# Scan stage of a two-layer hybrid backbone: loads and SiLUs issued from the scan steps

## The chip, the cores and the metric

The kernel is one program on one core of a Trainium2 chip. The metric is the device time of that core in microseconds (us), lower is better. The runs shown are whole executions; one further execution was recorded by the profiler, and every row below comes from that one.

## What is computed

Two layers over 1024 latent tokens and 256 context tokens, width 1024. Each layer projects the normed tokens into four mixers of 256 columns, concatenates their outputs, projects them back (`w_out`), and runs a squared-ReLU MLP. Only the mixers matter here:

```python
y_conv = silu(layer_norm(depthwise_conv(a * sigmoid(g)))) @ w_pw + b_pw
y_gla  = rms_norm(bidirectional_scan(gla)) * silu(r)
y_att  = softmax_attention(q, k, v)
y_ret  = rms_norm(bidirectional_scan(retention)) * silu(g)
x = x + g1 * (concat([y_conv, y_gla, y_att, y_ret]) @ w_out)
```

The second layer needs no context outputs, so its stage below has 8 token tiles of 128 and not 10.

## The kernel before, in words

All matrices are kept transposed, 128 features on the partitions and tokens along the free axis. A product in full precision is made of three products of halves (`mm3`, lines 190 to 195): `split` (line 180) casts a tile to a high half on ScalarE (line 181) and leaves the rest as a low half on VectorE (line 182). The program is Python that writes out every instruction; a scheduler then orders each engine's instructions by their place in the program and by when it reckons their inputs to be ready, so a load may be issued ahead of its place. All loads named here go through the one queue of SyncE (SP), in order.

**The scan stage** (lines 952 to 1112, once per layer) lies between the projections, which leave their results in DRAM, and the `w_out` matmuls. It runs as follows.

- `zc` (128 x 2 x 1280) holds the normed convolution outputs, `gt` (128 x 4 x 1280) the gates: columns 0 and 1 those of the gated linear attention (GLA, "g"), columns 2 and 3 those of the retention ("r"). `y[t]` collects the four mixers' outputs of token block t; its columns 4 and 5 are the attention's.
- Lines 971 to 984 allocate and load constants (`mc`, on POOL's queue, line 974) and the chunk states of both scans (`kvs`: `gkv`, `rkv`, line 982). Each of these tiles has one buffer (`bufs=1`).
- `states("g")` (line 986, drained at line 1012) is the serial recurrence over tiles: 16 VectorE operations at line 994 and four at line 999 that give `gs`, the decayed state that every GLA tile reads. `states("r")` does the same for the retention beside the scan.
- `scan_loads` (line 1005) loads one tile's queries and keys (`gx` or `rx`, line 1008) and values (`gv` or `rv`, line 1009), three buffers each; line 1013 issues the first three ahead. Line 1015 loads and splits the pointwise weights `pw`.
- Lines 1016 to 1026 issue the loads of `gt` columns 0 and 1, of `zc`, of `gt` columns 2 and 3, and of the attention outputs into `y[t][:, 4:6]`. Lines 1027 to 1036 apply SiLU to all of them but the attention's, on ScalarE (`act`, line 167, is the helper; the instruction is at line 175). `act` puts a table load ahead whenever the function wanted is in another table set than the last one: SiLU is in one set, the Ln and Exp of the tails in another.
- `scan_tile` (line 1038) does one tile: score matmuls into `sc`, a mask on VectorE (`gab`, lines 1054 and 1055; `rab`, line 1057), then into `oo` the products with the values and with the states. `scan_tail` (line 1079) norms a finished token block (ScalarE lines 1084, 1085 and 175, VectorE lines 1094 and 1096), multiplies by the gate and writes `y`.
- `pointwise` (line 954) splits 256 tokens of `zc` at a time (`shi`, `slo`), multiplies by `w_pw` and writes `y[t][:, 0:2]` (line 968).
- Line 1111 runs three streams in lockstep rounds, one step of each per round: the scans (GLA blocks first, then retention), `states("r")` and `pointwise()`. A block of n tiles takes n + 2 rounds, so the scans take 32 rounds in the first layer and 24 in the second; `pointwise` takes 10 and 8, from the first round on.

After the stage `w_out` (from line 1121) splits `y` and multiplies; its weight slabs (512 KB each) are loaded and split during the stage when queue and buffers allow.

Of the kernel before, what the change touches and what calls it, by code (L numbers as in the profile page):

```python
# [8 lines left out]
F32 = mybir.dt.float32  # L9
F32R = mybir.dt.float32r  # L10
I32 = mybir.dt.int32
AF = mybir.ActivationFunctionType
ALU = mybir.AluOpType
# [7 lines left out]
NTILE = NT // 128  # L21
CT = NCTX // 128
# [6 lines left out]
TOK = [(0, 256), (256, 512), (768, 512)]  # L29
# [45 lines left out]
CST, OFF = _consts()  # L75
# [25 lines left out]
def build(tc, a, out, dbg=None):  # L101
    cst = a["cst"]
    nc = tc.nc
# [33 lines left out]
    def cslice(name):  # L137
        o, n = OFF[name]
        return cst[:, o:o + n]
# [9 lines left out]
    glav = dram.tile([NTILE, 128, 256], F32, name="glav")  # L149
    glaf = dram.tile([NTILE, 128, 6, 128], F32, name="glaf")  # L150
    glakv = dram.tile([NTILE, 128, 128], F32, name="glakv")
    retv = dram.tile([NTILE, 128, 256], F32, name="retv")
    retf = dram.tile([128, 5, NT], F32, name="retf")
    retkv = dram.tile([NTILE, 128, 128], F32, name="retkv")
    yconv = dram.tile([128, 2, NT], F32, name="yconv")
    attraw = dram.tile([NTILE, 128, 320], F32, name="attraw")
    yatt = dram.tile([128, 2, NT], F32, name="yatt")
    gatedr = dram.tile([128, 4, NT], F32, name="gatedr")
# [8 lines left out]
    def act(out_, in_, func, want=None, **kw):  # L167
        if want == "anyexp":
            want = cur["set"] if cur["set"] in ("exp", "tanh") else "exp"
        if want is not None and want != cur["set"]:  # L170
            ld = nc.scalar.preload_act_table_set(sets[want]).ins
            for u_ in cur["users"]:
                after_(ld, u_)
            cur.update(set=want, users=[], load=ld)
        i_ = nc.scalar.activation(out_, in_, func, **kw).ins  # L175
        if want is not None:
            after_(i_, cur["load"])
            cur["users"].append(i_)

    def split(hi, lo, src):  # L180
        nc.scalar.copy(hi, src)  # L181
        nc.vector.tensor_tensor(lo, src, hi.bitcast(F32), op=ALU.subtract)  # L182
# [7 lines left out]
    def mm3(ps, pairs):  # L190
        n = len(pairs)
        for i, (lh, ll, rh, rl) in enumerate(pairs):
            mm(ps, lh, rh, i == 0, False)
            mm(ps, lh, rl, False, False)
            mm(ps, ll, rh, False, i == n - 1)

    def par(*streams):
        streams = [(iter(g), w, []) for g, w in streams]
        busy = True
        while busy:  # L200
            busy = False
            for gens, w, live in streams:
                while len(live) < w:
                    g = next(gens, None)
                    if g is None:
                        break
                    live.append(g)
                for g in list(live):
                    busy = True
                    if next(g, par) is par:  # L210
                        live.remove(g)
            yield
# [17 lines left out]
    def drain(g):  # L230
        for _ in g:
            pass
# [18 lines left out]
    def load_slab(src, k, n):  # L251
        wd_ = W["width"]
        st = W["st"].tile([128, wd_], F32, tag="wst", name="wst", bufs=W["stages"])
        if not isinstance(src, list):
            src = [(src, n)]
        o = 0
        v = st[:, :k * n].rearrange("p (k n) -> p k n", k=k)
        for s, w in src:
            nc.sync.dma_start(out=v[:, :, o:o + w], in_=s)
            o += w  # L260
        p = W["pools"][W["n"] // W["group"] % len(W["pools"])]
        W["n"] += 1
        hi = p.tile([128, wd_], F32R, tag="whi", name="whi")
        lo = p.tile([128, wd_], F32R, tag="wlo", name="wlo")
        split(hi[:, :k * n], lo[:, :k * n], st[:, :k * n])
        return (hi[:, :k * n].rearrange("p (k n) -> p k n", k=k), lo[:, :k * n].rearrange("p (k n) -> p k n", k=k))
# [20 lines left out]
    gdec = cpool.tile([128, NTILE, 2, 2], F32, name="gdec")  # L287
# [16 lines left out]
    def vec(l, name, i=0):  # L304
        o, _ = VROWS[name]
        return vecs[l][:, o + i:o + i + 1]
# [118 lines left out]
    b = bank()  # L425
# [43 lines left out]
    for l in range(2):  # L469
        last = l == 1  # L470
        tts = [1, 2] if last else [0, 1, 2]
# [194 lines left out]
        def tiles_of(t):  # L666
            o, n = TOK[t]
            return range(o // 128, (o + n) // 128)
# [75 lines left out]
        for half in range(2):  # L744
            sl = granule(l, [(C_CONV + 128 * half, 128), (C_CONV + 256 + 128 * half, 128)], 256)
            for t in tts:
                o, n = TOK[t]
# [10 lines left out]
        for q, c0 in enumerate((C_GATE_R, C_GATE_G)):  # L758
            sl = granule(l, [(c0, 256)], 256)
            for t in tts:  # L760
                o, n = TOK[t]
                for j in range(2):
                    b = colA(sl, j * 128, t)
# [178 lines left out]
        y = [None if last and t == 0 else xy_tile(t, "y") for t in range(3)]  # L942
# [4 lines left out]
        def bank2(tag):  # L947
            return psm.tile([128, 2, 512], F32, tag=tag, name=tag, bufs=2)

        open_w()  # L950
        mp = pools.get("mp", side="right", bufs=2, reuse_waits="tile")
        zc = mp.tile([128, 2, NT], F32, name="zc", bufs=1)
        gt = mp.tile([128, 4, NT], F32, name="gt", bufs=1)
        def pointwise():
            whi, wlo = pw
            for t in tts:
                for c in range(0, TOK[t][1], 256):
                    o = TOK[t][0] + c
                    shi = mp.tile([128, 2, 256], F32R, tag="shi", name="shi")
                    slo = mp.tile([128, 2, 256], F32R, tag="slo", name="slo")  # L960
                    split(shi, slo, zc[:, :, o:o + 256])
                    yield
                    bb = bank2("sc")
                    for d in range(2):
                        b = bb[:, d, :]
                        ds = slice(d * 128, (d + 1) * 128)
                        mm3(b[:, 0:256], [(whi[:, k, ds], wlo[:, k, ds], shi[:, k, :], slo[:, k, :]) for k in range(2)])
                        nc.scalar.activation(y[t][:, d, c:c + 256], b[:, 0:256], AF.Identity, bias=vec(l, "conv_b_pw", d))
                    yield

        mc = {}
# [14 lines left out]
        def states(nm):  # L986
            kv = kvs[nm]
            if nm == "g":
                nc.vector.tensor_tensor(gtot, gdec[:, :, :, 0], gdec[:, :, :, 1], op=ALU.mult)
            for n_ in range(1, NTILE - 1):  # L990
                for d_, od in enumerate((fwd, back)):
                    i, pr = od[n_], od[n_ - 1]
                    dec = gtot[:, i, d_:d_ + 1] if nm == "g" else mc["retdec"]
                    nc.vector.scalar_tensor_tensor(kv[:, i, d_, :], kv[:, pr, d_, :], dec, kv[:, i, d_, :],
                                                   op0=ALU.mult, op1=ALU.add)
                yield
            if nm == "g":
                for d_, i0, i1, p0 in ((0, 1, NTILE, 0), (1, 0, 1, 1), (1, 2, NTILE - 1, 3), (1, NTILE - 1, NTILE, 0)):
                    nc.vector.tensor_tensor(gs[:, i0:i1, d_, :], kv[:, p0:p0 + i1 - i0, d_, :],
                                            gdec[:, i0:i1, d_, d_:d_ + 1].to_broadcast([128, i1 - i0, 64]), op=ALU.mult)  # L1000
                yield
# [3 lines left out]
        def scan_loads(kind, i):  # L1005
            x = mp.tile([128, 6 if kind == "g" else 5, 128], F32, tag=kind + "x", name=kind + "x", bufs=3)
            v = mp.tile([128, 256], F32, tag=kind + "v", name=kind + "v", bufs=3)
            nc.sync.dma_start(out=x, in_=glaf[i] if kind == "g" else retf[:, :, i * 128:(i + 1) * 128])
            nc.sync.dma_start(out=v, in_=(glav if kind == "g" else retv)[i])
            ready[kind, i] = (x, v)  # L1010
# [5 lines left out]
        for q in range(0, 4, 2):  # L1016
            for t in tts:
                o, n = TOK[t]
                nc.sync.dma_start(out=gt[:, q:q + 2, o:o + n], in_=gatedr[:, q:q + 2, o:o + n])
            if q == 0:  # L1020
                for t in tts:
                    o, n = TOK[t]
                    nc.sync.dma_start(out=zc[:, :, o:o + n], in_=yconv[:, :, o:o + n])
        for t in tts:
            o, n = TOK[t]
# [75 lines left out]
        def scans():  # L1101
            for kind in ("g", "r"):
                for t in tts:
                    old = tails.pop() if tails else iter(())
                    for _ in scan_block(kind, t):
                        step(old)
                        yield
                    drain(old)
            drain(tails.pop())

        drain(par(([scans()], 1), ([states("r")], 1), ([pointwise()], 1)))
        pools.close("psm", "mp")
        if "y" in dbg and dbg.get("l", 0) == l:
            for t in tts:
# [156 lines left out]
```

## Time and profile before

| | us |
|---|---|
| three runs | 3226.3, 3220.46, 3217.87 |
| their median | 3220.46 |
| profiled execution, its own time | 3216.42 |
| its span, first to last instruction | 3214.7 |

The span is 1.7 us shorter than that execution's own time, and the execution is 4.0 us below the median. In the span the first layer's scan stage lies between about 645 and 755 us, the second's between about 2301 and 2402 us. "PEclk" in a row is the granted TensorE clock as a share of full speed; "DMA share" is how busy the 16 DMA engines were.

### The profile page before, as it was taken

The page shows a single profiled execution, that of the slowest core. Times are in us where ns is not written, and L with a number is a line of the kernel's source. Part 1 is how long each engine was busy: PE and PEld are TensorE (multiplying, and loading weights), DVE is VectorE, ACT ScalarE, POOL GpSimd, SP SyncE. Part 2 cuts the span into 40 slices and gives each one's busy share as a digit, 9 for nine tenths or more (in the row PEclk, how much of TensorE's full clock was granted, in tenths as well). Part 3 has the DMA queues.
Part 4 walks back from the last instruction along what each step waited for, and adds up shares of the span by engine and source line. Part 5 has one row for each costly group of instructions (what it writes and reads, how often), then busy time and mean ns, then how long its engine had stood idle before and what let it go on. Part 6 is the DMA issues. An engine that isn't in the chain of part 4 may idle for free. (4 is left out here: it accounts for less than half of the span.)

```text
span 3214.7 us, 43493 instructions
## 1 busy us (share of the span) xinstructions
PE 3026.1 (94%) x18101; PEld 2446.6 (76%) x18101; DVE 1671.4 (52%) x2660; ACT 913.3 (28%) x1650; POOL 66.6 (2%) x114
## 2 busy tenths in 40 slices
PE   7899899968999999999999799999779999999998
PEld 4777677646888888888888777687548888888887
DVE  5549634344655444454545659643444644444545
ACT  5223344243321111121112433343342321112222
POOL 0200000000000000000000010000000000000000
PEclk8899999979999999999999799999879999999999
DMA  8322412262122222221110310212531211111111
GB/s 273 112 70 86 129 44 79 84 216 95 60 79 86 86 86 79 82 63 40 40 40 1 99 55 30 80 48 65 174 117 70 66 46 46 40 53 53 53 40 53
DMA packets 267229, 250.31 MB, mean 78 GB/s; under 512 B 28258, under 2 KB 227512, under 8 KB 267032
## 3 DMA queue, kind: packets, MB, share of 16 engines
q1 hardware_dynamic: 266616, 246.61, 24.4%
q8 instruction: 142, 2.33, 0.3%
q0 software_dynamic: 416, 0.92, 0.1%
q14 instruction: 55, 0.45, 0.0%
HBM read 200.42 MB, written 47.05 MB: 77 GB/s over the span
## 5 line engine op out<-in xcount | busy, mean ns | idle before, releaser
L188 PE MATMUL bank<-ahi,whi 128*128 128x512 f32 (+1 forms) x2096 | 788.2, 376 | 14.4 <-ACT ahi L181 11.2
L188 PE MATMUL bank<-ahi,wlo 128*128 128x512 f32 (+1 forms) x2096 | 778.7, 372 | 2.0 <-DVE wlo L182 2.0
L188 PE MATMUL bank<-alo,whi 128*128 128x512 f32 (+1 forms) x2096 | 780.0, 372 | 0.0
L1184 DVE SCALAR_TENSOR_TENSOR x<-bank,mods,x 128x512 f32<-128x512 f32 (+1 forms) x640 | 438.8, 695 | 247.6 <-PE bank L188 246.1
L188 PEld LDWEIGHTS bank<-ahi,whi 128*128 128x128 f32 x2096 | 398.2, 190 | 102.4 <-issue 13.7
L188 PE MATMUL bank<-hl,whi 128*128 128x512 f32 (+1 forms) x1280 | 471.8, 369 | 0.0
L188 PE MATMUL bank<-hh,whi 128*128 128x512 f32 (+1 forms) x1280 | 471.3, 368 | 0.0
L188 PE MATMUL bank<-hh,wlo 128*128 128x512 f32 (+1 forms) x1280 | 471.0, 368 | 0.0
L188 PEld LDWEIGHTS bank<-ahi,wlo 128*128 128x128 f32 x2096 | 397.5, 190 | 72.8 <-issue 5.9
L188 PEld LDWEIGHTS bank<-alo,whi 128*128 128x128 f32 x2096 | 398.2, 190 | 68.0 <-issue 5.4
L181 ACT CAST whi<-wst 128x1024 fp32r<-128x1024 f32 (+2 forms) x226 | 199.9, 895 | 663.8 <-PE bank L188 483.9
L182 DVE TENSOR_TENSOR wlo<-wst,whi 128x1024 fp32r<-128x1024 f32 (+2 forms) x226 | 231.6, 1036 | 264.5 <-ACT whi L181 262.2
L1168 ACT ACTIVATE tmp<-bank 128x512 f32<-128x512 f32 (+1 forms) x160 | 88.3, 553 | 647.2 <-PE bank L188 646.3
L188 PEld LDWEIGHTS bank<-hl,whi 128*128 128x128 f32 x1280 | 241.4, 189 | 40.1 <-issue 0.2
L188 PEld LDWEIGHTS bank<-hh,whi 128*128 128x128 f32 x1280 | 241.4, 189 | 40.0
L188 PEld LDWEIGHTS bank<-hh,wlo 128*128 128x128 f32 x1280 | 241.3, 189 | 40.1 <-issue 0.2
L1170 DVE TENSOR_TENSOR tmp<-tmp 128x512 f32<-128x512 f32 (+1 forms) x160 | 102.0, 639 | 304.8 <-ACT hh L1169 303.0
L188 PE MATMUL bank<-whi,ahi 128*128 128x256 f32 (+2 forms) x640 | 197.7, 310 | 12.3 <-ACT gqk L857 5.3
L188 PE MATMUL bank<-wlo,ahi 128*128 128x256 f32 (+2 forms) x640 | 192.3, 300 | 0.2 <-DVE wlo L182 0.2
L188 PE MATMUL bank<-whi,alo 128*128 128x256 f32 (+2 forms) x640 | 191.4, 299 | 0.0
L521 DVE SCALAR_TENSOR_TENSOR yacc<-u,wdw,yacc 128x1295 f32<-128x1295 f32 (+1 forms) x120 | 168.4, 1420 | 0.8
L691 DVE TENSOR_REDUCE amx<-S 128x1 f32<-128x1280 f32 (+1 forms) x72 | 98.8, 1372 | 130.7 <-PE S L188 125.5
(214 smaller groups left out, 3090.1 us busy)
## 6 DMA issues: line engine op xcount, KB each, us to landing
wm<-in_w_mod_dram SPq DMA_DIRECT2D x64, 512.0 KB, 3.8
wst<-in_w_up_dram SPq DMA_DIRECT2D x64, 512.0 KB, 4.0
wst<-in_w_down_dram SPq DMA_DIRECT2D x64, 512.0 KB, 4.2
wm<-in_w_mod_dram SPq DMA_DIRECT2D x64, 256.0 KB, 3.0
wst<-in_w_in_dram SPq DMA_DIRECT2D x48, 256.0 KB, 2.8
wst<-in_w_out_dram SPq DMA_DIRECT2D x16, 512.0 KB, 4.7
x<-xdram SPq DMA_DIRECT2D x4, 2048.0 KB
glaf<-gf SPq DMA_DIRECT2D x18, 384.0 KB, 2.3
```

Source lines behind the costliest of these rows:

```text
L181: nc.scalar.copy(hi, src)
L182: nc.vector.tensor_tensor(lo, src, hi.bitcast(F32), op=ALU.subtract)
L188: nc.tensor.matmul(ps, lhsT=lhsT, rhs=rhs, start=start, stop=stop)
L521: nc.vector.scalar_tensor_tensor(yv, uv, wv, yv, op0=ALU.mult, op1=ALU.add)
L691: nc.vector.reduce_max(mx[:, 0:1], S[:, 0:nk * 128], axis=AX.X)
L1168: nc.scalar.activation(rl[:, :n], b[:, :n], AF.Relu)
L1170: nc.vector.tensor_tensor(rl[:, :n], rl[:, :n], rl[:, :n], op=ALU.mult)
L1184: nc.vector.scalar_tensor_tensor(xt[t][:, d, :], b[:, :n], mod(l, 5, d, seg), xt[t][:, d, :], op0=ALU.mult, op1=ALU.add)
```

## The change

It inserts 95 lines into the scan stage behind line 1022 and exchanges the third stream of line 1111. The inserted lines are, in order: a SiLU of `gt` columns 0 and 1 and a `break` out of the loop that loads `gt`; a generator `later()`; then a second text of `pointwise`, of the allocations and loads of `mc` and `kvs`, of `states`, `ready` and `scan_loads`, of the draining of `states("g")`, of the first three `scan_loads`, of `pw` and of the loop that loads `gt` and `zc`. The only line taken out is the old line 1111. So the first text of these statements runs (up to the `break`), then the second text runs after it, and behind it the old lines 1023 to 1036, with all their loads and SiLUs, stand unchanged; `later()` issues loads and SiLUs of `zc`, of `gt` columns 2 and 3 and of the attention outputs once more, one load per round, and then hands over to `pointwise`. `ready` starts empty again in the second text, so the first three `gx` and `gv` tiles of the first text have no reader. Tiles of one name share their buffers: the second `gkv` takes the buffer of the first.

```diff
         for q in range(0, 4, 2):
             for t in tts:
...
                 nc.sync.dma_start(out=gt[:, q:q + 2, o:o + n], in_=gatedr[:, q:q + 2, o:o + n])
             if q == 0:
                 for t in tts:
                     o, n = TOK[t]
+                    act(gt[:, 0:2, o:o + n], gt[:, 0:2, o:o + n], AF.Silu, "silu")
+                break
+
+        def later():
+            for t in tts:
+                o, n = TOK[t]
+                nc.sync.dma_start(out=zc[:, :, o:o + n], in_=yconv[:, :, o:o + n])
+                yield
+            for t in tts:
+                o, n = TOK[t]
+                nc.sync.dma_start(out=gt[:, 2:4, o:o + n], in_=gatedr[:, 2:4, o:o + n])
+                yield
+            for t in tts:
+                o, n = TOK[t]
+                for hf in range(2):
+                    act(zc[:, hf, o:o + n], zc[:, hf, o:o + n], AF.Silu, "silu", bias=vec(l, "conv_ln_b", hf),
+                        scale=vec(l, "conv_ln_g", hf))
+            for t in tts:
+                o, n = TOK[t]
+                act(gt[:, 2:4, o:o + n], gt[:, 2:4, o:o + n], AF.Silu, "silu")
+            for t in tts:
+                o, n = TOK[t]
+                nc.sync.dma_start(out=y[t][:, 4:6, :], in_=yatt[:, :, o:o + n])
+                yield
+            yield from pointwise()
+
+        def pointwise():
...
+        for nm, src in (("g", glakv), ("r", retkv)):
+            kvs[nm] = mp.tile([128, NTILE, 2, 64], F32, name=nm + "kv", bufs=1)
+            nc.sync.dma_start(out=kvs[nm].rearrange("p i d c -> p i (d c)"), in_=src.rearrange("i p c -> p i c"))
...
+        drain(states("g"))
+        for i in [i_ for t in tts for i_ in tiles_of(t)][:3]:
+            scan_loads("g", i)
+        pw = load_slab(a["conv_w_pw"][l].rearrange("(k p) n -> p k n", p=128), 2, 256)
+        for q in range(0, 4, 2):
+            for t in tts:
+                o, n = TOK[t]
+                nc.sync.dma_start(out=gt[:, q:q + 2, o:o + n], in_=gatedr[:, q:q + 2, o:o + n])
+            if q == 0:
+                for t in tts:
+                    o, n = TOK[t]
                     nc.sync.dma_start(out=zc[:, :, o:o + n], in_=yconv[:, :, o:o + n])
         for t in tts:
             o, n = TOK[t]
...
-        drain(par(([scans()], 1), ([states("r")], 1), ([pointwise()], 1)))
+        drain(par(([scans()], 1), ([states("r")], 1), ([later()], 1)))
```

## Rows read from the trace of the kernel before

**Rows 1.** The page's first part: busy time and share of the span by engine.
```profile
PE 3026.1 (94%) x18101; PEld 2446.6 (76%) x18101; DVE 1671.4 (52%) x2660; ACT 913.3 (28%) x1650; POOL 66.6 (2%) x114
```

**Rows 2.** Chain that ended last, second layer's stage: start us, us, what.
```profile
2302.57 8.13 DMA gx<-glaf
2310.72 7.00 DMA zc<-yconv
2317.74 1.53 ACT zc L175 x2
...
2319.96 6.67 PE sc L188 x20
```

**Rows 3.** Busy time by 5 us, first layer's stage; last: PEclk, DMA share, GB/s.
```profile
645.00:650.00 5.00, 0.00 (x0) 0.00 (x0) 0.18 (x1) 0.00 (x0) 0.00 (x0) 0.50 0.90 239
...
655.00:660.00 5.00, 1.26 (x12) 0.93 (x16) 4.45 (x17) 2.48 (x4) 0.00 (x0) 0.50 1.07 393
...
665.00:670.00 5.00, 4.44 (x16) 3.09 (x16) 2.11 (x3) 3.41 (x7) 0.00 (x0) 0.50 0.88 298
```

**Rows 4.** SP's queue in order of time, first layer: start us, us, issue.
```profile
644.63 0.43 SPq L982 DMA_DIRECT2D gkv<-glakv  x1
...
651.89 1.80 SPq L1019 DMA_DIRECT2D gt<-gatedr  x3
...
660.56 0.33 SPq L1008 DMA_DIRECT2D gx<-glaf  x1
```

**Rows 5.** DVE in order of time, first layer.
```profile
649.82 3.22 DVE L994 SCALAR_TENSOR_TENSOR gkv<-gkv,gtot 128x64 f32<-128x64 f32 x16 [6.58 <-DMA gkv<-glakv]
652.96 1.56 DVE L999 TENSOR_TENSOR gs<-gkv,gdec 128x576 f32<-128x576 f32 x4
...
658.58 0.68 DVE L182 TENSOR_TENSOR wlo<-wst,whi 128x512 fp32r<-128x512 f32 x1
```

**Rows 6.** DMA issues by kind, both layers together: KB each, us to landing.
```profile
gx<-glaf SPq DMA_DIRECT2D x18, 384.0 KB, 4.3
...
gt<-gatedr SPq DMA_DIRECT2D x8, 512.0 KB, 6.5
...
gv<-glav SPq DMA_DIRECT2D x18, 128.0 KB, 3.9
...
zc<-yconv SPq DMA_DIRECT2D x4, 512.0 KB
...
gkv<-glakv SPq DMA_DIRECT2D x2, 640.0 KB
...
wst<-in_conv_w_pw_dram SPq DMA_DIRECT2D x2, 256.0 KB, 2.8
```

**Rows 7.** PE in order of time, first layer.
```profile
652.85 2.08 PE L188 MATMUL sc<-gx 64*128 64x256 f32 x8 [8.99 <-DMA gx<-glaf]
...
659.79 0.71 PE L188 MATMUL oo<-gx,gs 64*64 64x128 f32 x8
...
667.94 0.41 PE L188 MATMUL sc<-slo,whi 128*128 128x256 f32 x1
...
678.06 0.28 PE L188 MATMUL sc<-slo,whi 128*128 128x256 f32 x1
...
754.95 0.79 PE L188 MATMUL bank<-ahi,whi 128*128 128x256 f32 x2 [5.48 <-ACT ahi L181]
```

**Rows 8.** ACT in order of time, first layer.
```profile
656.49 0.62 ACT L181 CAST whi<-wst 128x512 fp32r<-128x512 f32 x1 [12.25 <-DMA gt<-gatedr]
...
659.79 1.06 ACT L175 ACTIVATE gt<-gt 128x1024 f32<-128x1024 f32 x1 [0.31 <-DMA gt<-gatedr]
660.75 1.08 ACT L175 ACTIVATE zc<-zc,vec 128x256 f32<-128x256 f32 x2
...
662.39 2.92 ACT L175 ACTIVATE zc<-zc,vec 128x512 f32<-128x512 f32 x4
...
672.45 1.28 ACT L171 ACT_TABLE_LOAD   x1
```

More of the change, by code (lines that the diff above doesn't have):

```diff
@@ new lines, in pointwise @@
+        def pointwise():
+            whi, wlo = pw
+            for t in tts:
+                for c in range(0, TOK[t][1], 256):
+                    o = TOK[t][0] + c
+                    shi = mp.tile([128, 2, 256], F32R, tag="shi", name="shi")
+                    slo = mp.tile([128, 2, 256], F32R, tag="slo", name="slo")
+                    split(shi, slo, zc[:, :, o:o + 256])
+                    yield
+                    bb = bank2("sc")
+                    for d in range(2):
+                        b = bb[:, d, :]
+                        ds = slice(d * 128, (d + 1) * 128)
+                        mm3(b[:, 0:256], [(whi[:, k, ds], wlo[:, k, ds], shi[:, k, :], slo[:, k, :]) for k in range(2)])
+                        nc.scalar.activation(y[t][:, d, c:c + 256], b[:, 0:256], AF.Identity, bias=vec(l, "conv_b_pw", d))
+                    yield
@@ new lines, in build @@
+        mc = {}
+        for nm in ("mlt", "mdg", "retm", "retdec", "blk64"):
+            mc[nm] = mp.tile([128, OFF[nm][1]], F32, name="c_" + nm, bufs=1)
+            nc.gpsimd.dma_start(out=mc[nm], in_=cslice(nm))
+        mlt = mc["mlt"].bitcast(I32)[:, None, None, :].to_broadcast([128, 2, 2, 128])
+        mdg = mc["mdg"][:, None, None, :].to_broadcast([128, 2, 2, 128])
+        fwd = list(range(NTILE))
+        back = list(range(CT - 1, -1, -1)) + list(range(NTILE - 1, CT - 1, -1))
+        kvs = {}
@@ new lines, in build, with states @@
+        for nm, src in (("g", glakv), ("r", retkv)):
+            kvs[nm] = mp.tile([128, NTILE, 2, 64], F32, name=nm + "kv", bufs=1)
+            nc.sync.dma_start(out=kvs[nm].rearrange("p i d c -> p i (d c)"), in_=src.rearrange("i p c -> p i c"))
+        gtot = mp.tile([128, NTILE, 2], F32, name="gtot", bufs=1)
+        gs = mp.tile([128, NTILE, 2, 64], F32, name="gs", bufs=1)
+        def states(nm):
+            kv = kvs[nm]
+            if nm == "g":
+                nc.vector.tensor_tensor(gtot, gdec[:, :, :, 0], gdec[:, :, :, 1], op=ALU.mult)
+            for n_ in range(1, NTILE - 1):
+                for d_, od in enumerate((fwd, back)):
+                    i, pr = od[n_], od[n_ - 1]
+                    dec = gtot[:, i, d_:d_ + 1] if nm == "g" else mc["retdec"]
+                    nc.vector.scalar_tensor_tensor(kv[:, i, d_, :], kv[:, pr, d_, :], dec, kv[:, i, d_, :],
+                                                   op0=ALU.mult, op1=ALU.add)
+                yield
+            if nm == "g":
+                for d_, i0, i1, p0 in ((0, 1, NTILE, 0), (1, 0, 1, 1), (1, 2, NTILE - 1, 3), (1, NTILE - 1, NTILE, 0)):
+                    nc.vector.tensor_tensor(gs[:, i0:i1, d_, :], kv[:, p0:p0 + i1 - i0, d_, :],
+                                            gdec[:, i0:i1, d_, d_:d_ + 1].to_broadcast([128, i1 - i0, 64]), op=ALU.mult)
+                yield
@@ new lines, in build, with scan_loads @@
+        ready = {}
+        def scan_loads(kind, i):
+            x = mp.tile([128, 6 if kind == "g" else 5, 128], F32, tag=kind + "x", name=kind + "x", bufs=3)
+            v = mp.tile([128, 256], F32, tag=kind + "v", name=kind + "v", bufs=3)
+            nc.sync.dma_start(out=x, in_=glaf[i] if kind == "g" else retf[:, :, i * 128:(i + 1) * 128])
+            nc.sync.dma_start(out=v, in_=(glav if kind == "g" else retv)[i])
+            ready[kind, i] = (x, v)
+        drain(states("g"))
+        for i in [i_ for t in tts for i_ in tiles_of(t)][:3]:
+            scan_loads("g", i)
@@ L1023, in build @@
+        pw = load_slab(a["conv_w_pw"][l].rearrange("(k p) n -> p k n", p=128), 2, 256)
[4 more added lines that the diff above has]
+            if q == 0:
+                for t in tts:
+                    o, n = TOK[t]
                     nc.sync.dma_start(out=zc[:, :, o:o + n], in_=yconv[:, :, o:o + n])
```

## The prediction

> **What bounds the kernel now.** I read the shares by engine first: PE is busy 94% of the span [rows 1], so outside a few stages only PE work counts, and the change touches none of it. The scan stage is one of the exceptions. The chain of waits for the second layer's stage begins with two DMA waits, 8.13 us for the first `gx` and 7.00 us for `zc`, then the SiLU of `zc` (1.53 us) and 6.67 us of matmuls [rows 2]. (The chain that the profile follows does not reach back to the first layer; there I go by the engines' own order of time.) The windows of 5 us say what that wait is made of: in the first layer PE does nothing from 645 to 650 us and 1.26 us of work from 655 to 660, at a granted clock of 0.50 (the 1.2 GHz level), while the DMA engines are full, 1.07 at 393 GB/s [rows 3]. The head of the stage is bounded by bytes in a queue; the rest of it is a chain of short steps on PE, DVE and ACT.
>
> **What the change is.** Its words say that loads are spread. The diff takes nothing out of the head: the old loads and SiLUs stand, a second text of the head runs behind the first, and `later()` adds a third set. So I cost additions, with one thing moved: `pointwise` starts nine rounds later in the first layer (three loads each of `zc`, `gt`, `y`), six in the second.
>
> **Bytes added.** Sizes are from [rows 6], halved for 256-token blocks. Head, first layer: `gkv` and `rkv` 2 x 640 KB, three `gx` and `gv` 3 x 512 KB, `pw` 256 KB, `gt` columns 0 and 1 1280 KB; together 4352 KB = 4.46 MB. Second layer: `gt` has 1024 KB, together 4.19 MB. `later()`: three loads of 1280 KB, 3.93 MB, and three of 1024 KB, 3.15 MB. All: 15.7 MB, which at 393 GB/s is 40 us of full DMA.
>
> **The head (term A).** Two waits run side by side. First the states: the second `gkv` uses the buffer of the first and must wait until the first `gs` is done, 652.96 + 1.56 = 654.5 us [rows 5]. The first `gkv` took 649.82 - 644.63 = 5.2 us from issue to its reader [rows 4, 5]; the reload lands at 659.7 at best, and the recurrence (3.22) and `gs` (1.56) run again, so `gs` is ready at 664.5. Its first reader starts at 659.79 today [rows 7]: +4.7 us at least. Second the queue: the first `gx`, `gv`, `pw` and `gt` (3.15 MB, 8 us at 393 GB/s) are in the rings ahead of it, and all that lies behind, the second `gx`, `zc`, the second halves of `gt` and the fourth tile's `gx` (issued at 660.56 today, [rows 4]), comes later by 4.46 MB / 393 GB/s = 11.4 us; second layer 10.7 us. The bounds are 4.7 and 11.4 us; I take 10 and 9, near the upper one, since the DMA is full exactly there. The repeated DVE work (3.22 + 1.56, `wlo` 0.68) is inside that wait: DVE has nothing else to do.
>
> **Relief (term B).** In the present order `pointwise` fills PE at the low clock just behind the head: its 256-column matmuls take 0.41 us there and 0.28 us later [rows 7]. Moved back, they leave that stretch to the scan tiles, and `zc` no longer holds the chain: at most 7.00 + 1.53 = 8.5 us per layer [rows 2], at least nothing, as the second `gx` now arrives when `zc` used to. `pointwise` must then run among the later tiles. I take -3 us each.
>
> **`later()` (term C).** Its loads need 3.93 / 393 = 10.0 us and 8.0 us of DMA. They lie behind the head, where the DMA is still 0.88 busy [rows 3], ahead of tiles whose `gx` each needs. A reload of `zc` waits for the SiLU of the same place, which comes late itself; SP is in order, so the `gx`, `gv` and `w_out` loads behind it wait with it, and PE for those. Bounds 0 and 10.0 (8.0); I take 4 and 3, under half, because three tile buffers run ahead.
>
> **SiLUs (term D).** Added on ACT in the first layer: a cast 0.62, `gt` columns 0 and 1 about 2.7, `zc` 1.08 + 2.92 = 4.0, `gt` columns 2 and 3 about 2.7 (two of 1.06 and half of that) [rows 8]: 10 us, 8 in the second layer. ACT waited 12.25 us before its first cast, so the early ones cost nothing if it stays that idle; without that cover they delay the first tail by up to 3 us. The 6.7 us of `later()` come in one block in round six, behind the first tail's Ln and Exp (round five); the next tail waits. Price 0 to 6.7 us per layer, I take 1. The block also returns to SiLU's table set and back, two more table loads of 1.28 us [rows 8] in the first layer, 2.6 us, of which I put 2 on the path. In the second layer the block comes in round four, before any tail, and costs no load.
>
> The Trainium skill (ScalarE: Activation LUTs, What ACT_TABLE_LOAD costs and Rules for kernel authors) speaks against such a block: do all of one set before switching, at about 2.66 us a switch with its drain. By the page the two loads are an estimated 5.3 us and the sum would be 2.7 us higher; the row shows 1.28 and decides.
>
> **At no cost:** POOL's second constants (POOL is busy 2% of the span, [rows 1]; they go out early) and 38 more issues on SP at 0.33 to 0.6 us each [rows 4]: the DMA engines are the limit, not the issue; if that cover were gone, 17 us over two layers.
>
> **Sum.** First layer 10 - 3 + 4 + 1 + 2 = 14, second 9 - 3 + 3 + 1 = 10: +24 us. Against the profiled execution 3216.4 + 24 = 3240.4; that stands 4.0 us below the median, so 3244.5 us, 3244 rounded. A measurement of this kernel can tell about 0.3%, 9.7 us, from no change.
>
> **Rivals.**
> - *All of it on the path.* The stage becomes DMA-bound and ACT-bound: A 11.4 + 10.7, C 18.0, D 2.6 + 13.4, no relief: +56 us, 3276 us. For: in-order SP, waits chained through reload, SiLU, reload. Against: from 0.88 at 665 us the DMA share falls off later, and 8.13 us was the longest DMA wait [rows 2, 3]. Chance 0.18 (for +38 and more).
> - *Hidden.* A at its lower bound (4.7 twice) is met by relief of about as much, C and D lie beside: 0 to +9 us, about 3225. For: tiles one and two need only buffers already loaded, and the low-clock stretch loses its other user. Against: DVE and ACT behind the head also wait for bytes. Chance 0.12.
> - *Faster.* The chain through `zc` [rows 2] is the only thing that bounds the head, and the repeated loads fit in the wait that is there: relief 8.5 per layer against 4.7, 2 x (4.7 - 8.5) = -8, with the clock up earlier -10 or more: 3210 us. It decides if the second `gkv` and `gx` land by about 660 us, and `pointwise` finds idle PE among later tiles. Against: 393 GB/s shows no room for 3 MB more by then. Chance 0.06.
>
> That the change doesn't do what it says is my forecast's own ground, not a rival.
>
> **Numbers.** Forecast (+10 to +38) 0.64. The range reaches from 3227 (A nearly at its lower bound, a good part of the hidden case) to 3274 (nearly all of the first rival), leaving out some 0.15 below and 0.05 above. Slower 0.64 + 0.18 = 0.82, same 0.12, faster 0.06.
>
> **What would show it.** Right: two `gkv` loads and 32 operations of the `gkv` recurrence per layer, the first `oo` matmul with `gs` 5 to 10 us further behind the first `gkv` issue than now, 3.9 MB of `later()` in the rings before the GLA tiles end, two more table loads in the first layer, `w_out` starting (754.95 now, [rows 7]) some 14 us later. Wrong: the first `oo` no later than now, or `pointwise` lengthening the retention part by more than the head loses; or a gain outside the stages.

## The result and the profile after

The changed kernel took 3240.22 us (median of four runs, 3238.54 to 3247.27) against 3219.16 us for the kernel before in as many runs beside it: ratio 1.0076, 95% interval 1.0059 to 1.0094, so it is slower by about 0.8%. (The quotient of the two medians is 1.0065, +21 us, inside that interval.) Its profiled execution took 3240.76 us, with a span of 3239.0 us against 3214.7: +24.3 us.

The page's first part, its HBM totals and the table loads of the kernel after:

```profile
span 3239.0 us, 43634 instructions
...
PE 3029.4 (94%) x18101; PEld 2447.5 (76%) x18101; DVE 1682.0 (52%) x2704; ACT 932.3 (29%) x1674; POOL 71.7 (2%) x124
...
HBM read 217.07 MB, written 47.05 MB: 82 GB/s over the span
```
```profile
L171 ACT ACT_TABLE_LOAD  x12: 1283/1283/1283, 0.7 to 2361.7; - x12
```

PE does the same 18101 matmuls in almost the same busy time [rows 1]; DVE has 44 instructions more, ACT 24, two of them table loads (ten before). HBM reads grow from 200.42 to 217.07 MB, 16.65 MB more: the 15.7 MB of the prediction and the second constants. Nothing was taken away.

Where the 24 us are is read from the order of time on PE in each stage. All times here are us behind the stage's first `gkv` issue:

| | first layer: first `oo` with `gs` | last GLA `oo` | `w_out` starts | second layer: first `oo` | last GLA `oo` | `w_out` |
|---|---|---|---|---|---|---|
| before | 15.2 | 68.1 | 110.3 | 16.8 | 59.9 | 101.4 |
| after | 27.7 | 81.2 | 132.1 | 27.0 | 66.6 | 106.8 |

The first stage is 21.8 us longer and the second 5.4 us. (The first begins 0.85 us later, and the work behind the two stages is 2.3 and 1.4 us shorter: 21.8 + 5.4 + 0.85 - 3.7 = 24.3.) Cut at the marks, the first stage loses 12.5 us before its first `oo`, 0.6 in the rest of the GLA tiles and 8.7 in the retention part; the second loses 10.2, then wins back 3.5 and 1.3.

**The head.** SP's queue of the kernel after, first layer (start us, us, issue; beside [rows 4]):

```profile
645.48 0.43 SPq L982 DMA_DIRECT2D gkv<-glakv  x1
...
655.16 0.36 SPq L1077 DMA_DIRECT2D gkv<-glakv  x1
655.56 2.18 SPq L1077 DMA_DIRECT2D rkv<-retkv  x1
657.78 3.67 SPq L1103 DMA_DIRECT2D gx<-glaf  x1
...
675.22 6.89 SPq L1029 DMA_DIRECT2D zc<-yconv  x3
682.15 1.26 SPq L1033 DMA_DIRECT2D gt<-gatedr  x2
683.52 0.41 SPq L1103 DMA_DIRECT2D gx<-glaf  x1
```

The windows of 5 us (beside [rows 3]; at the end granted clock, DMA share, GB/s):

```profile
655.00:660.00 5.00, 0.00 (x0) 0.00 (x0) 0.69 (x1) 1.72 (x3) 0.00 (x0) 0.50 1.07 385
660.00:665.00 5.00, 0.00 (x0) 0.00 (x0) 1.80 (x10) 1.60 (x2) 0.00 (x0) 0.50 1.17 312
665.00:670.00 5.00, 3.79 (x16) 2.54 (x16) 5.00 (x24) 0.28 (x1) 0.00 (x0) 0.50 1.06 399
```

And PE in order of time (beside [rows 7]):

```profile
666.20 3.79 PE L188 MATMUL sc<-gx 64*128 64x256 f32 x16 [21.50 <-DMA gx<-glaf]
672.12 1.12 PE L188 MATMUL oo<-gab,gv 128*64 128x128 f32 x8 [2.13 <-DVE gab L1150]
673.17 0.70 PE L188 MATMUL oo<-gx,gs 64*64 64x128 f32 x8
...
689.63 2.08 PE L188 MATMUL sc<-gx 64*128 64x256 f32 x8 [5.13 <-DMA gx<-glaf]
...
777.56 0.80 PE L188 MATMUL bank<-ahi,whi 128*128 128x256 f32 x2 [5.48 <-ACT ahi L181]
```

The second `gkv` goes out 9.7 us behind the first; until 665 us the rings are full and PE does nothing. PE's wait for its first `gx` grew from 8.99 to 21.50 us. Three tiles later it waits again, 5.13 us, for a `gx` that SP issued only at 683.52: the three reloads of `zc` ahead of it held SP for 6.89 us, since each has to wait until the SiLU of the same place is done (ACT's first rows of `zc` below end at 675.19, 679.63 and 681.56 us).

**DVE and ACT.** DVE's order of time (beside [rows 5]) has the recurrence twice, and ACT's (beside [rows 8]) the second block of SiLUs between two more table loads:

```profile
650.18 3.22 DVE L994 SCALAR_TENSOR_TENSOR gkv<-gkv,gtot 128x64 f32<-128x64 f32 x16 [6.10 <-DMA gkv<-glakv]
653.32 1.56 DVE L999 TENSOR_TENSOR gs<-gkv,gdec 128x576 f32<-128x576 f32 x4
...
663.20 3.22 DVE L1089 SCALAR_TENSOR_TENSOR gkv<-gkv,gtot 128x64 f32<-128x64 f32 x16 [4.33 <-DMA gkv<-glakv]
666.34 1.56 DVE L1094 TENSOR_TENSOR gs<-gkv,gdec 128x576 f32<-128x576 f32 x4
667.81 2.83 DVE L1089 SCALAR_TENSOR_TENSOR rkv<-rkv,c_retdec 128x64 f32<-128x64 f32 x14
670.55 0.69 DVE L1149 TENSOR_TENSOR gab<-sc,c_mdg 128x512 f32<-128x512 f32 x1
```
```profile
674.11 1.08 ACT L175 ACTIVATE zc<-zc,vec 128x256 f32<-128x256 f32 x2
...
678.11 1.52 ACT L175 ACTIVATE zc<-zc,vec 128x512 f32<-128x512 f32 x2
...
680.05 1.51 ACT L175 ACTIVATE zc<-zc,vec 128x512 f32<-128x512 f32 x2
...
686.65 1.28 ACT L171 ACT_TABLE_LOAD   x1
687.95 3.91 ACT L175 ACTIVATE zc<-zc,vec 128x256 f32<-128x256 f32 x6
691.76 2.50 ACT L175 ACTIVATE gt<-gt 128x512 f32<-128x512 f32 x3
...
694.79 1.28 ACT L171 ACT_TABLE_LOAD   x1
```

These rows say what ends the head. In the kernel after, DVE works without a gap from 663.20 us to the mask `gab` for which the first `oo` matmuls wait: the second recurrence, `gs`, most of the retention's recurrence, the mask. In the kernel before the order was the same, with this row between `gs` and the mask:

```profile
654.43 2.83 DVE L994 SCALAR_TENSOR_TENSOR rkv<-rkv,c_retdec 128x64 f32<-128x64 f32 x14
```

The first `oo` with `gs` starts 659.79 - 649.82 = 9.97 us behind the start of the recurrence before [rows 5, 7], and 673.17 - 663.20 = 9.97 us behind the start of the second one after; the second layer has the same 9.97 us in both kernels. So all 12.5 us of the first layer are the later landing of the `gkv` that is used: its issue came 9.7 us behind the first one's, and its reader started 8.0 us after that issue, where before it was 5.2. `gx` was only a little earlier: the first tile's scores were there at about 668.1 us (half of the 3.79 us row, an estimate), 2.4 us before DVE came to the mask.

The chain that ended last, second layer (start us, us, what; beside [rows 2]):

```profile
2321.12 5.71 DMA gkv<-glakv
2326.92 3.22 DVE gkv L994 x16
2330.14 1.48 DVE gs L999 x4
2331.65 6.40 DMA gkv<-glakv
2338.14 3.22 DVE gkv L1089 x16
```

Load, recurrence, `gs`, load, recurrence: the chain that went through `gx` and `zc` now goes twice through the states.

### The profile page after: what moved, and what is told of

The parts are those of the page before. It is cut to its first block, busy times and chain, and to the rows that moved or that the text cites. A ratio compares the mean times of both kernels' runs of the same rounds, so it can differ in the third digit from the quotient of the medians.

```text
span 3239.0 us, 43634 instructions
## 1 busy us (share of the span) xinstructions
PE 3029.4 (94%) x18101; PEld 2447.5 (76%) x18101; DVE 1682.0 (52%) x2704; ACT 932.3 (29%) x1674; POOL 71.7 (2%) x124
## 3 DMA queue, kind: packets, MB, share of 16 engines
HBM read 217.07 MB, written 47.05 MB: 82 GB/s over the span
## 4 chain that ended last, share of the span: by engine, by line
PE 86%; DMA 4%; DVE 4%; ACT 3%; SPq 1%; issue 1%; POOL 0%; DVEq 0%; ACTq 0%; POOLq 0%
PE bank L188 71%; PE ob L188 3%; PE S L188 3%; PE pt L185 3%; PE s L188 3%; PE sc L188 1%; PE oo L188 1%; PE mo L188 1%; SPq L324 1%; DMA wm<-in_w_mod_dram 0%; DVE alo L387 0%; DMA wst<-in_w_in_dram 0%; DMA gx<-glaf 0%; PE s L185 0%; ACT whi L181 0%
```

## The experiments

Three theories stood at the start. T1 is the sum of the prediction: most of the loss is the repeated head (A), the late `pointwise` gives some back (B), `later()` costs a little (C, D). T2: the waits that `later()` puts into SP and ACT are the main part. T3: the late start of `pointwise` is. Later T1 was split: in the head either the chain of states (T1a) or the queue of bytes (T1b) decides. Ratios are to the kernel before, measured beside each on the same chip, with 95% intervals; 0.1% is 3.2 us.

**1. The change without `later()`.**
```diff
-        drain(par(([scans()], 1), ([states("r")], 1), ([later()], 1)))
+        drain(par(([scans()], 1), ([states("r")], 1), ([pointwise()], 1)))
```


> The changed kernel with the third stream back to the old pointwise stream: later() is never run, so the repeated head (states, first tiles, pw, gt columns 0 and 1, their SiLU) stands alone. Theory 1 (the repeated bytes and states at the head are the loss, term A without relief): +19 us against the kernel before, and the first layer's stage about as much longer as the second's. Theory 2 (the reloads of later() behind their SiLUs block SP's queue and are the main loss): under +10 us. Theory 3 (pointwise put back into the retention part is the loss): +10 to +12 us, the head's part of it alone.

Measured: 1.0062 [1.0050, 1.0074], +20 us; first `oo` at 27.3 and 27.2 us. The repeated head alone costs about what term A said (19), and most of what the whole change costs. By stage it was 15.0 and 9.1 us, where about the same in both layers had been expected.

**2. `later()` alone.** The kernel before, with `later()` (all of its loads and SiLUs) as third stream and no second head.
```diff
-        drain(par(([scans()], 1), ([states("r")], 1), ([pointwise()], 1)))
+        drain(par(([scans()], 1), ([states("r")], 1), ([later()], 1)))
```


> The kernel before with later() as the third stream and no repeated head: reloads of zc, gt columns 2 and 3 and the attention outputs, their SiLUs a second time, pointwise nine and six rounds later. Theory 1: terms C + D - B = 7 + 4 - 6 = +5 us. Theory 2: +14 us or more, nearly all of it in the first layer, with SP seen waiting for the SiLU of zc. Theory 3: about +12 us, as in the run with pointwise late alone.

Measured: 1.0018 [1.0007, 1.0028], +6 us (2 to 9), as B + C + D said (+5); T2 (+14 or more) and T3 (+12) lie outside, so neither is the main cause. By stage: the first 12.3 us longer, the second 1.6 shorter, in a profiled execution that was the longest of twelve (3229.45 us, median 3223.76). What T2 had in mind is there all the same, without any second head: the three reloads of `zc` hold SP for 6.79 us, and PE waits 5.93 us for the fourth tile's `gx`.

```profile
661.67 6.79 SPq L1041 DMA_DIRECT2D zc<-yconv  x3
```
```profile
676.77 2.08 PE L188 MATMUL sc<-gx 64*128 64x256 f32 x8 [5.93 <-DMA gx<-glaf]
```

**3. `pointwise` late, nothing else.**
```diff
+        def pw_late():
+            for _ in range(3 * len(tts)):
+                yield
+            yield from pointwise()
...
-        drain(par(([scans()], 1), ([states("r")], 1), ([pointwise()], 1)))
+        drain(par(([scans()], 1), ([states("r")], 1), ([pw_late()], 1)))
```


> The kernel before with pointwise alone begun nine (first layer) and six rounds later; no load or SiLU added. Theory 1: term B, -6 us over two layers (relief of the low-clock stretch). Theory 2: between -6 and 0 us. Theory 3: +8 us or more, with the retention part longer by as much in the first layer.

Measured: 0.9981 [0.9970, 0.9992], -6 us: term B, and a kernel faster than both. But not by layer: the second stage is 6.5 us shorter, the first 3.0 us longer; there the GLA part wins 5.5 us and the retention part, into which `pointwise` moves, loses 9.0 (51.2 against 42.2 us from the last GLA `oo` to `w_out`). That loss is in every profile: with the late stream in the first layer (the change and experiments 2 to 5 and 9 to 12) this part takes 50.8 to 53.1 us, without it (the kernel before and experiments 1, 6, 7 and 8) 42.1 to 43.7.

**4. What the words of the change say.** The loads of `zc`, of `gt` columns 2 and 3 and of the attention outputs, and their SiLUs, stand in `later()` only; the head loads `gt` columns 0 and 1 and nothing is repeated.
```diff
-                    nc.sync.dma_start(out=zc[:, :, o:o + n], in_=yconv[:, :, o:o + n])
...
+        for t in tts:
+            o, n = TOK[t]
+            act(gt[:, 0:2, o:o + n], gt[:, 0:2, o:o + n], AF.Silu, "silu")
+
+        def later():
+            for t in tts:
...
+                nc.sync.dma_start(out=zc[:, :, o:o + n], in_=yconv[:, :, o:o + n])
+                yield
```


> What the words of the change say and no more: no repeated head, the loads and SiLUs of zc, gt columns 2 and 3 and the attention outputs only in later(). Theory 1: the head loses 2.62 MB (6.7 us of DMA at 393 GB/s) in the first layer and 2.10 MB in the second, the relief stays, the two table loads in the first layer stay: -8 to -10 us. Theory 2: no reload waits for a SiLU, so SP is free: -10 us. Theory 3: the retention part takes back what the head gains: 0 to +5 us.

Measured: 0.9992 [0.9983, 1.0001], -3 us: T1 (-8 to -10) and T2 (-10) are not borne out, and T3's 0 lies at the edge of the interval. T3's mechanism is in the profile: the first layer's retention part took 53.0 us, 10.8 more than before. And the head gained next to nothing (first `oo` at 14.8 us, 15.2 before). The SP queue shows that the loads did not leave the head:

```profile
648.03 1.80 SPq L1018 DMA_DIRECT2D gt<-gatedr  x3
650.20 1.84 SPq L1026 DMA_DIRECT2D zc<-yconv  x3
652.09 1.11 SPq L1030 DMA_DIRECT2D gt<-gatedr  x2
656.63 0.33 SPq L1008 DMA_DIRECT2D gx<-glaf  x1
```

Five of these six loads, written one per round, went out back to back behind the first `gt`, ahead of the fourth tile's `gx`: nothing held them, so the scheduler issued them at once. They were not spread. The first stage was 9.5 us longer than before (119.9), the second 6.7 shorter, and the SiLU block still cost two table loads.

**5. The same, with the SiLUs ahead of the first tail.** All loads of `zc` in round one, of `gt` in round two, the SiLUs in round three (ten table loads again), `pointwise` from the same round as in experiment 4.
```diff
                 nc.sync.dma_start(out=zc[:, :, o:o + n], in_=yconv[:, :, o:o + n])
-                yield
+            yield
...
+            for _ in range(2 * len(tts) - 2):
+                yield
...
             yield from pointwise()
```


> As the run that does only what the words of the change say, but the SiLUs of zc and of gt columns 2 and 3 come in the third round, before the first tail's Ln and Exp, so the two added table loads of the first layer go; pointwise keeps its late start. Theory 1 (the block between the tails and its two table loads cost the first layer what it lost there against pointwise late alone, 119.9 - 113.3 = 6.6 us): about -8 us against the kernel before, first layer's stage near 113 us. Rival (the first layer's loss is pointwise in the retention part and the clock there, not the block): no better than -3 us, stage near 120 us.

Measured: 0.9987 [0.9975, 0.9999], -4 us: between the theories, and not to be told from experiment 4. In the profiles the first stage is shorter (111.7 against 119.9 us) and the second 3.2 us longer; two executions of one kernel differ by 4 us in the first (experiment 9), so that is a hint at most.

**6. `pointwise` late in the second layer only.**
```diff
-            for _ in range(3 * len(tts)):
+            for _ in range(3 * len(tts) if last else 0):
```


> The kernel before with pointwise begun six rounds later in the second layer alone; the first layer as it was. Theory 1 (relief belongs to the second layer, where the stage fell from 101.4 to 94.9 us; the first lost 3.0): -6 to -9 us. Rival (the difference between the layers was where the granted clock happened to fall, and no property of the layers): -3 to -5 us, or a second layer's stage that no longer is near 95 us.

Measured: 0.9983 [0.9972, 0.9994], -5 us, second stage 94.8 us (94.9 in experiment 3, 101.4 before). The time does not decide between the theories, the stage does: the relief is the second layer's; late in the first layer as well gives nothing more that can be told.

**7. Of the head, only the states twice.** Experiment 1 without the first text's `scan_loads`, `pw`, `gt` and SiLU, so that these are done once; what is still done twice are `mc`, `kvs` and the recurrence.
```diff
-        for i in [i_ for t in tts for i_ in tiles_of(t)][:3]:
-            scan_loads("g", i)
-        pw = load_slab(a["conv_w_pw"][l].rearrange("(k p) n -> p k n", p=128), 2, 256)
-        for q in range(0, 4, 2):
...
-                break
```


> The run with the repeated head alone, cut to the repeated constants, chunk states and their recurrence: the second gkv must wait for the first recurrence, but no gx, gv, pw or gt is loaded twice and no SiLU of gt columns 0 and 1 is done twice. Theory 1a (the serial wait: reload 5.2, recurrence 3.2, gs 1.6 us behind the first gs): first GLA product with the states 4 to 6 us later per layer, +9 us in all. Theory 1b (only bytes count: 1.31 MB per layer at 393 GB/s): +6.7 us. Rival (hidden behind gx and the masks): 0 to +3 us.

Measured: 1.0031 [1.0019, 1.0043], +10 us (6 to 14), which fits T1a (+9) but does not exclude T1b (+6.7). The rows are T1a's. PE in order of time, first layer:

```profile
656.88 1.12 PE L188 MATMUL oo<-gab,gv 128*64 128x128 f32 x8 [3.38 <-DVE gab L1138]
662.31 0.70 PE L188 MATMUL oo<-gx,gs 64*64 64x128 f32 x8 [4.30 <-DVE gs L1082]
```

The `sc` products and the masks are in time; the first `oo` with `gs` waits 4.30 us for the second `gs`. Against before it comes 3.6 and 4.0 us later in the two layers, a little under the lower bound of 4.7.

**8. Of the head, only the bytes twice.** Experiment 1 without the second `mc`, `kvs`, `states` and its draining; what stays are the second `gx`, `gv`, `pw`, `gt` and one SiLU.
```diff
-        kvs = {}
-        for nm, src in (("g", glakv), ("r", retkv)):
-            kvs[nm] = mp.tile([128, NTILE, 2, 64], F32, name=nm + "kv", bufs=1)
...
-        drain(states("g"))
```


> The run with the repeated head alone, cut the other way: constants, states and recurrence once, but the first three gx and gv, pw and gt columns 0 and 1 loaded twice, with the SiLU and the cast twice. Theory 1b (bytes in the queue: 3.15 MB in the first layer and 2.88 MB in the second at 393 GB/s): +15 us, first score matmul 8 and 7 us later. Theory 1a (the state wait is the larger part of the head): +6 to +10 us.

Measured: 1.0044 [1.0029, 1.0059], +14 us, as T1b said (+15); the first score matmul came 7.6 and 5.5 us later (8 and 7 expected). PE in order of time, first layer:

```profile
659.18 2.08 PE L188 MATMUL sc<-gx 64*128 64x256 f32 x8 [16.57 <-DMA gx<-glaf]
...
663.86 0.70 PE L188 MATMUL oo<-gx,gs 64*64 64x128 f32 x8
```

Here the `sc` products are late (16.57 us of waiting for `gx`) and `gs` is not. Both halves of term A exist. In time 10 + 14 = 24 stand against 20 together, a difference within the intervals (4 to 5 us either way for each). At the first `oo` of the first layer the halves do not overlap: 3.6 and 5.3 us alone, 12.1 together (experiment 1), because there the second `gkv` lands behind the first text's bytes.

**9. The changed kernel once more,** beside the next three.

> The changed kernel once more, as the measure for the three runs beside it: +24 us against the kernel before (1.0076). A second profile also shows whether the split between the layers (first stage +21.8 us, second +5.4) belongs to the kernel or to one execution.

Measured: 1.0090 [1.0075, 1.0105], +29 us; the stages 25.7 and 6.8 us longer than before. The uneven split repeats.

**10. The change without the SiLUs of `later()`.**
```diff
-                for hf in range(2):
-                    act(zc[:, hf, o:o + n], zc[:, hf, o:o + n], AF.Silu, "silu", bias=vec(l, "conv_ln_b", hf),
-                        scale=vec(l, "conv_ln_g", hf))
...
-                act(gt[:, 2:4, o:o + n], gt[:, 2:4, o:o + n], AF.Silu, "silu")
```


> The changed kernel without the SiLUs of later(): zc and gt columns 2 and 3 are loaded again and used without SiLU, so the output is not the reference's. Loads and order stay. Theory 1 (term D as priced, 1 + 2 in the first layer and 1 in the second): +20 us against the kernel before. Theory D2 (the block between two tails with its two table loads costs the first layer about 8 us, as the step from 119.9 to 111.7 us of its stage between the two spread runs suggests): +15 us, first layer's stage near 124 us. Rival (ACT has room for it): +24 us.

Measured: 1.0078 [1.0064, 1.0091], +25 us, 4 less than the whole change beside it, with some 6 either way; ten table loads; first stage 132.5 us, within the whole change's two values (132.1 and 136.0). Term D was 4, the rival 0, and the noise does not tell them apart; D2 (9 less, a first stage near 124) is not borne out. The SiLUs are no main part. The fourth tile's `gx` still goes out 37.6 us behind the first `gkv`.

**11. The change without the three reloads of `later()`.** The SiLUs run twice on the same data.
```diff
-                nc.sync.dma_start(out=zc[:, :, o:o + n], in_=yconv[:, :, o:o + n])
...
-                nc.sync.dma_start(out=gt[:, 2:4, o:o + n], in_=gatedr[:, 2:4, o:o + n])
...
-                nc.sync.dma_start(out=y[t][:, 4:6, :], in_=yatt[:, :, o:o + n])
```


> The changed kernel without the reloads of later(): the SiLUs of zc and of gt columns 2 and 3 are done twice on the same values, so the output is not the reference's. Theory 1 (term C as priced, 4 + 3): +17 us against the kernel before. Theory 2 (the reloads wait in SP's queue for SiLUs and hold the fourth tile's gx behind them, seen as 6.89 us for three issues): +12 us or less, with the fourth tile's gx issued some 6 us earlier behind the first gkv. Rival (bytes hidden beside the scan): +24 us.

Measured: 1.0045 [1.0027, 1.0063], +14 us; against the whole change beside it the reloads are worth 0.0045, 14 us, with some 7 either way (the intervals of 0.0018 and 0.0015 together give 0.0023). The rival (bytes hidden, +24) is out. Its SP queue:

```profile
644.03 0.43 SPq L982 DMA_DIRECT2D gkv<-glakv  x1
...
667.49 1.63 SPq L1111 DMA_DIRECT2D gt<-gatedr  x3
672.08 0.33 SPq L1100 DMA_DIRECT2D gx<-glaf  x1
```

The fourth tile's `gx` goes out 28.0 us behind the first `gkv`; in the whole change 683.52 - 645.48 = 38.0. With experiment 10, which left it at 37.6, this puts the hold on the reloads and not on the second SiLUs: what a reload waits for is the first SiLU of its place. In the first layer the GLA tiles behind the first `oo` take 47.2 us here, against 53.5 and 57.4 in the two profiles of the whole change; the retention part is the same.

**12. The second states in each other's buffer.** The second `gkv` takes the buffer of the first `rkv`, so that it need not wait for the first `gs`.
```diff
-            kvs[nm] = mp.tile([128, NTILE, 2, 64], F32, name=nm + "kv", bufs=1)
+            kvs[nm] = mp.tile([128, NTILE, 2, 64], F32, name=nm + "kv", tag={"g": "rkv", "r": "gkv"}[nm], bufs=1)
```


> The changed kernel with the buffers of the second gkv and rkv exchanged, so that the second gkv waits for no recurrence, only for the first load of rkv. Bytes and work are the same. Theory 1b (in the full change the second gx and its bytes end the head, the state wait lies beside them): +22 to +24 us. Theory 1a (the state wait ends the head): +18 us, the first GLA product with the states some 4 us earlier per layer.

Measured: 1.0075 [1.0062, 1.0089], +24 us, not to be told from experiment 9. The edit hardly did what it was for:

```profile
640.22 0.43 SPq L982 DMA_DIRECT2D gkv<-glakv  x1
...
649.33 0.36 SPq L1077 DMA_DIRECT2D gkv<-glakv  x1
```

The second `gkv` still goes out 9.1 us behind the first (9.7 in the whole change), behind the `gt` loads; in the second layer it is 8.7 against 10.5 us. The first `oo` of the first layer still follows 9.97 us behind the start of the second recurrence, at 27.2 us. So in the full head the states come last, as in T1a, but two things hold their reload to about the same time, and taking one of them away gains next to nothing: without the wait for the first `gs` it goes out at 9.1 us (here), with few loads ahead of it at 9.6 us (experiment 7, the end of the first `gs`), with both at 9.7. What the bytes add, as in T1b, is the landing: the reader starts 8.0 us after the issue in the whole change and 5.1 us after it in experiment 7. A buffer of its own, at an earlier place in the queue, was not tried.

## Why the prediction was right, and where its steps were off

The forecast was +24 us; the two measurements gave +24 (1.0076) and +29 (1.0090), the profiled execution +24.3. The time of 3240 us lies in the range. Its ground, that the diff removes nothing and repeats the head, is what the traces show. Step by step:

- **A, the head: right in size, the picture only in part.** Predicted 10 + 9 = 19, measured 20 alone (experiment 1, 4 either way). The first `oo` was to come 5 to 10 us later; it came 12.5 and 10.2 later, where the queue's upper bounds were 11.4 and 10.7. The prediction let two waits run side by side and took nearly the longer one. The rows show them one behind the other: the second `gkv` goes out at the end of the first `gs`, lands late behind the first text's bytes (its reader starts 8.0 us after the issue, 5.1 in experiment 7), and recurrence, `gs`, the retention's recurrence (2.83 us) and the mask follow on DVE. The 4.7 us of the lower bound leave out these last two, which lay between `gs` and its first reader before as well. And 393 GB/s was taken for all of the added bytes; from 660 to 665 us the full rings moved 312.
- **B, relief: right in sum, wrong by layer.** Predicted -3 and -3, measured -6 in all (experiment 3). The step that failed is that `pointwise` "must then run among the later tiles" at no price: in the first layer those are retention tiles, and the part from the last GLA `oo` to `w_out` grew by 9.0 us in experiment 3 and by 8.7 in the change. That is less than the head lost, so the mark named for a wrong forecast was not reached. Why the second layer does not pay this is not shown.
- **C, the reloads: mechanism right, size probably too low.** Predicted 7. Taken out of the change they are worth 14, with some 7 either way, so that 7 lies at the edge; from experiments 2, 3 and 10, 6 + 6 - 4 = 8, no surer. By the profiles the first layer's GLA tiles pay 6 to 10 us (experiment 11), where 4 was predicted. "Under half, because three tile buffers run ahead" was the failing reason: the three buffers were used up when the fourth `gx` went out 38.0 us into the stage, and PE waited 5.13 us for it. It is not the long head that does this, as PE waited 5.93 us without it (experiment 2). Nor did all of the reloads lie behind the head: the attention outputs of the first layer, a third of its bytes, went out again at 621.50, 631.94 and 639.89 us, before the stage began.
- **D, the SiLUs: size not settled.** Predicted 4, measured 4 with some 6 either way, so neither 4 nor nothing is shown; the rival's 16 us are not borne out. The next SiLU starts 1.30 us behind the start of a table load (686.65, 687.95), so no drain beyond the row's 1.28 us is seen; the 2.66 us of the Trainium skill (ScalarE: Activation LUTs, What ACT_TABLE_LOAD costs) is not what this trace shows.
- **By layer: wrong.** Predicted 14 and 10, `w_out` "some 14 us later"; measured 21.8 and 5.4, then 25.7 and 6.8. By the first profile B is the larger part of the error (6 of the first layer's 8, 3.5 of the second's 4.6). That the errors of the layers cancel in the sum is luck.
- **The rivals.** "All of it on the path" would have shown +38 or more. "Hidden" had the repeated head fit into idle time: experiment 1 alone costs 20. "Faster" had the chain through `zc` as the only bound: with the head repeated, PE's first `gx` came 12.5 us later. Its idea was right where no bytes are added (experiments 3 and 6).

The terms measured one by one give 20 - 6 + 14 + 4 = 32, with some 11 either way, against 24 to 29 for the whole. Whether they overlap is within the noise.

## What to carry to other kernels

Read a diff for what it leaves standing: here the loads that were to be spread stayed where they were, and the repeated ones were the cost. A load that this kernel's reordering scheduler found ready went out at once, whatever step it was written in (experiment 4), and a reload into a place still in use puts a wait into an in-order queue that holds every load behind it (experiments 2 and 11). Read each stage by itself: here starting one stream later helped one layer and not the other, and doing that there alone beats the kernel before by about 5 us (experiment 6).

## What the runs showed of the hardware that was not expected

Full rings are not a fixed rate: while the second states were loaded, whose source lies in runs of 512 bytes (128 values of four bytes), the DMA engines were busier (1.17) and moved less (312 GB/s) than just before and after (385 and 399 at 1.07 and 1.06). The first load of the states looks alike: 0.90 at 239 GB/s in the kernel before [rows 3], 1.10 at 287 from 645 to 650 us in experiment 7. That the piece size is the cause was not tried by itself.

The granted clock stayed at 0.50, the 1.2 GHz level, as long as PE idled in the head, and it fell again late in the first stage, around a wait of 2.20 us of PE for an `rx` that ended at 748.71 us. Two windows of the kernel after, and the same four matmuls in each:

```profile
720.00:740.00 20.00, 18.45 (x148) 12.11 (x146) 9.86 (x14) 9.34 (x14) 0.00 (x0) 0.95 0.32 97
740.00:760.00 20.00, 15.91 (x143) 8.85 (x144) 4.13 (x8) 4.48 (x5) 0.00 (x0) 0.74 0.43 127
```
```profile
730.39 1.98 PE L188 MATMUL sc<-fsq,c_blk 128*128 128x512 f32 x4
...
755.03 3.78 PE L188 MATMUL sc<-fsq,c_blk 128*128 128x512 f32 x4
```

The same work took 1.98 us in the window with a mean of 0.95 and 3.78 us in the one with 0.74, about the ratio of the two levels. So a part of the first layer's loss in the retention part is clock and not work. It is the smaller part: in experiments 1 and 7, with the work as before, this part had a mean granted clock of 0.84 and 0.85 (0.94 before) and took 1.5 us longer, while with the late stream, at 0.82 in the change, it took 8.7 longer, and PE was busy in it for 36.1 us against 26.8.
